# Low parts of the feed-forward gate and up weights made by an accumulating DMA

## The chip, the cores and the metric

The kernel runs on one core of one Trainium2 chip. The metric is the device time of one launch in microseconds; the kernel before took 1728.72 us, the median of three runs.

## The reference

Two layers of an encoder over 512 tokens of 1024 channels. Each layer mixes the tokens in four branches, adds and normalises, and then runs a gated feed-forward network of inner width 2816. The change lies in the feed-forward network alone:

```python
D_FF = ((8 * D_MODEL // 3 + 255) // 256) * 256      # 2816
for l in range(DEPTH):                               # DEPTH = 2
    ...
    x = _layer_norm(DEEPNORM_ALPHA * x + mixed @ w_out[l], ln1_g[l], ln1_b[l])
    ffn = (jax.nn.silu(x @ w_ffn_gate[l]) * (x @ w_ffn_up[l])) @ w_ffn_down[l]
    x = _layer_norm(DEEPNORM_ALPHA * x + ffn, ln2_g[l], ln2_b[l])
```

All operands are float32.

## The kernel before, in words

Every large product is made of three: each float32 operand is split into a high part, rounded to the type fp32r, and a low part, the rest, and TensorE (PE) adds high x high, high x low and low x high in one PSUM bank. The split of a weight tile of 128 x 1024 is done when it is loaded (`wload`, L308): SP issues a DMA into a float32 buffer `wr` (2 buffers), ScalarE (ACT) copies it to `wh` (the high part, 3 buffers), and VectorE (DVE) subtracts, `wl = wr - wh` (3 buffers). `split` (L173) is this pair of instructions. Almost all instructions of the profile carry line 121, that of the recorder through which they are emitted, so groups are told apart by tile names.

The feed-forward network of a layer takes 44 such tiles of `wgu`, gate and up columns in turn. `gemm_t` (L335) makes one tile's product, [128 features, 512 tokens] in the bank `pg`: 24 matmuls, eight with `wh` and XH, eight with `wh` and XL, and the last eight with `wl` and XH, where XH and XL are the two parts of the transposed input. So `wh` is needed from a tile's start, and `wl` from its last third on; the buffer of `wl` is free again when the tile ends. Three PSUM banks turn over: tile n takes the bank of tile n - 3.

The first three tiles (0 to 2) are emitted together by one `gemm_ts`, in two halves of tokens, since the last quarter of the tokens is still being normalised. From tile 3 on each is a `gemm_t` of its own. For each pair f of tiles (gate 2f, up 2f + 1) ACT makes silu of the gate in `fs`, DVE multiplies it by the up product, and the result is split into `gh` and `gl` for the down projection.

GpSimd (POOL) has three kinds of work there. `rows()` (L432), emitted at f = 1: 16 products and sums of 128 x 512 that scale and shift the rows of x for the residual, behind the last square root of the layer norm. In layer 0 alone, `s5_constants` (emitted at f = 0): a chain of small operations on the tables `ea` and `eb`, which begins when ACT has made sines of a table `s5w` of DVE. And, in layer 0 alone, eight times `s5_table` (L290; f = 4, 6, ... 18): six operations of 128 x 512 on `er`, `ei` and `et`, whose results SP stores.

Each engine runs its instructions in the order in which they stand. A scheduler makes that order; what is emitted under `tc.high_priority()` (the splits of weights) is put ahead of other work as soon as it can be placed.

Of the kernel before, what the change touches and what calls it, by code (L numbers as in the profile page):

```python
# [29 lines left out]
# columns of the constant table  # L30
C_ID, C_PERM, C_M, C_MASK, C_IND, C_HALF = 0, 128, 256, 384, 640, 642
C_N = 644
# columns of the per-layer table of per-partition parameters
# [5 lines left out]
# 2 KB slots of SBUF per partition: in general, gates on hold, sums over branches  # L39
# [3 lines left out]
# how work is interleaved: steps between S5's states and its outputs, tiles of gates on hold,  # L43
# backlog of VectorE (us) up to which S5 goes on, assumed latency between engines and of DMA (us)
# [7 lines left out]
class Pace:  # L52
    """a rough clock of the engines, kept while instructions are emitted: what has been emitted
    on each engine until when, and when each tile will be there. It only decides the order in
    which independent work is emitted"""
# [40 lines left out]
    def ring(self, tag, bufs, x):  # L96
        """a tile that takes the place of the one bufs before it"""
        r = self.rings.setdefault(tag, [])
        r.append(x.name)
        if len(r) > bufs:  # L100
            self.last["ring", x.name] = self.last.get(r[-1 - bufs], 0.0) + 0.15

    def ready(self, need):
        """when products of these tiles can start; None: not known yet"""
        if callable(need):
            return need()
        return max([self.when(x) for x in need], default=0.0)


class Metered:  # L110
    """an engine whose instructions advance the clock"""
# [21 lines left out]
def trunk_kernel(ctx: ExitStack, tc: tile.TileContext, xn, xt, wt, w2, wbr, wo, wgu, wdn,  # L133
# [48 lines left out]
    def three(pairs):  # L182
        """the three products of two split operands that carry float32's bits"""
        (ah, al), (bh, bl) = pairs
        return ((ah, bh), (ah, bl), (al, bh))

    # ---------------------------------------------------------------- constants
# [17 lines left out]
    # 0.5 * gate and GLU biases, for sigmoid(z) = (tanh(z/2) + 1) / 2  # L205
    hb = cp.tile([P, L, 36], F32, name="hb")

    # ------------------------------------------------------------------ S5 constants
    def s5_constants(l):
        """of a layer's 8 state tiles: decay, coefficient (exp(lambda dt) - 1) / lambda, and  # L210
        exp(i theta n) for n = 0..31 and n = 32 * (0..15)"""
# [15 lines left out]
        # theta * 2^k, reduced by multiples of 2 pi (exact products of short parts)  # L227
# [39 lines left out]
        # powers of exp(i theta), by doubling  # L267
# [22 lines left out]
    def s5_table(j, tabs):  # L290
        """exp(i theta n), n = 0..511, of a state tile"""
        v3 = lambda a: a.rearrange("p (a b) -> p a b", b=32)
        s3 = [P, 16, 32]
        er, ei, tm, tn = slot("er"), slot("ei"), slot("et"), slot("et")
        ar, ai = (bc(x[:, j, :].unsqueeze(2), s3) for x in tabs[0:2])
        br_, bi_ = (bc(x[:, j:j + 1, :], s3) for x in tabs[2:4])
        G.tensor_tensor(v3(er), ar, br_, ALU.mult)
        G.tensor_tensor(v3(tm), ai, bi_, ALU.mult)
        G.tensor_tensor(er, er, tm, ALU.subtract)
        G.tensor_tensor(v3(ei), ar, bi_, ALU.mult)  # L300
        G.tensor_tensor(v3(tn), ai, br_, ALU.mult)
        G.tensor_tensor(ei, ei, tn, ALU.add)
        return er, ei

    # ------------------------------------------------------------- weight streams
# [16 lines left out]

    def wload_s(src):
        """the same into slots, in halves"""
        hs, ls = [slot("wsh", F32R) for _ in range(2)], [slot("wsl", F32R) for _ in range(2)]
        r = wp.tile([P, 1024], F32, tag="wr", name=nm("wr"), bufs=2)
        pace.ahead = True
        SP.dma_start(r, src)
        with tc.high_priority():
            for i in range(2):  # L330
                split(hs[i], ls[i], r[:, 512 * i:512 * i + 512])
        pace.ahead = False
        return hs, ls

    def gemm_t(src, s, late=None):  # L335
        """[128 features, 512 tokens] = (weight tile)^T x^T, in PSUM"""
        return gemm_ts([src], s, late)[0]

    def gemm_ts(srcs, s, late=None):
        wl = [wload(x) for x in srcs]  # L340
        pss = [mm_ps(s) for _ in srcs]
        for (t0, t1) in (((0, 256), (256, S)) if late else ((0, S),)):
            for i, ((h, l), ps) in enumerate(zip(wl, pss)):
                if late and t0 == 0 and i == len(wl) - 1:
                    late()
                n = 0
                for w, xx in ((h, XH), (h, XL), (l, XH)):
                    for k in range(8):
                        T.matmul(ps[:, t0:t1], w[:, P * k:P * k + P], xx[:, k, t0:t1],
                                 start=(n == 0), stop=(n == 23))  # L350
                        n += 1
        return pss

    def gemm_n(srcs, width, pre=None, late=None):
        """four [128 tokens, width] = x (weight columns), in PSUM"""
# [24 lines left out]
    # ---------------------------------------------------------------- layer norm  # L380
    def layer_norm(l, w_, xh, pss, gt, bt, t, last):
        """x = LN(ALPHA x + psum) of one token tile, in place, the scale and shift left
        out; returns what is to be emitted later: x^T, split, and the scale and shift in rows"""
# [48 lines left out]
        def rows():  # L432
            """the same in rows, for the residual"""
            for h in range(2):
                G.tensor_tensor(xh[h], xh[h], gt[h], ALU.mult)
                G.tensor_tensor(xh[h], xh[h], bt[h], ALU.add)
# [3 lines left out]
    def proj_ln(l, w_, lh, ll, nk, wsrc, kl, ks, xh, gt, bt, last):  # L440
        """x = LN(ALPHA x + a w): a^T split in lh/ll (nk k-tiles), w streamed by rows;
        returns what is left to do for the last token tile"""
# [43 lines left out]
    # -------------------------------------------------------------------- mixers  # L486
    def silu_of(ps):
        """2 * silu, in SBUF"""
# [5 lines left out]
    def head_norm(src, o):  # L494
        """o = src normalised over each 64 of its 512 columns"""
# [93 lines left out]
    def spread(hl, order):  # L589
        """the two parts of a split operand to DRAM, in the order of a stack"""  # L590
# [5 lines left out]
    def fetch(x, r0):  # L596
        """32 rows from r0 of each of three operands, one below the other: one product of 96
        rows then stands for three of 32"""
        r = slot("skr")
        SP.dma_start(r[0:96, :], x[:, r0:r0 + 32, :])  # L600
        return r
# [68 lines left out]
    def gla_in(pss):  # L670
        """evacuate gk | gv | ga of the four token tiles"""
# [11 lines left out]
    def gla(l, gk, ga, gv, qf, gate2, br):  # L683
# [8 lines left out]
        # q * dk^-0.5, split, with the odd / even chunks zeroed  # L692
# [73 lines left out]
    def s5(l, s5c, uspr, br):  # L766
        # input and output matrices: b block-diagonal, c times the coefficient
# [68 lines left out]
        def states(j, cp4, m1, m2, m3, m4):  # L836
# [4 lines left out]
            # x = E y (m1 = re, m3 = im), then split  # L841
# [67 lines left out]
    def spare(*need):  # L909
        """once VectorE has little left to do"""  # L910
        return lambda: max(pace.at["V"] - SPARE, pace.ready(need))

    def gate_stream(l, order, brs, mix):
        """the gated sum over the branches, in steps: tanh(z / 2) of a tile of gates, or, when
        the branch's output is there, its product with the branch's matrix, gated and added"""
# [11 lines left out]
        def branch(bi, i, first, last):  # L927
# [14 lines left out]
            if last:  # L942
                # mixed = acc / 2, split
# [15 lines left out]
        while nb < len(todo):  # L959
# [9 lines left out]
            # matrices of the branches: loaded two pairs of tiles ahead, split one ahead  # L969
# [10 lines left out]
    def run(fill, *gens):  # L980
        """emit the generators' steps: of the first one that TensorE would not wait for,
        otherwise of fill, otherwise of the one that it would wait for least"""
# [17 lines left out]
    # -------------------------------------------------------------------- layers  # L1000
    rest = None
    for l in range(L):
        tt_ = lambda i, s: gemm_t(wt[l, i], s)
        # wt tiles: rq rk rg rg aq aq ak ak gq gr gr su su, then the gates
# [67 lines left out]
        # feed-forward  # L1072
# [3 lines left out]
        for f in range(NF):  # L1076
            if f > 0:
                ps += [gemm_t(wgu[l, i], "pg") for i in range(max(3, 2 * f), 2 * f + 2)]
# [18 lines left out]
# --------------------------------------------------------------- host-side layout  # L1097
def _tiles(w):
    """[.., K, N] -> [.., N/128, 128, K]: per tile of 128 columns, k-tiles side by side"""
# [8 lines left out]
def _constants():  # L1108
# [13 lines left out]
    # rotary tables, [128 = 4 heads x 32, 512]  # L1122
# [3 lines left out]
    # with the retention decay: queries times gamma^n, keys times gamma^-m dk^-0.5  # L1126
# [5 lines left out]
    # what the decay lacks in the blocks of 128 keys and their own 128 queries, [key, head x query]  # L1132
# [6 lines left out]
def _layout(inp):  # L1139
# [20 lines left out]
    wb = _tiles(a["w_branch"])  # [L, 4, 8, 128, 256]  # L1160
# [19 lines left out]
    # attention bias of the last 256 keys of a query tile  # L1180
# [9 lines left out]
    # b: rows = three copies of the 32 channels of tile j, columns [j][re | im][state]  # L1190
    sb = np.zeros((L, 3, 2, 16, 8, 2, 2, 64), f)  # L, copy, group, ch, j, re/im, group, state
    sc = np.zeros((L, 2, 64, 2, 8, 2, 16), f)     # L, group, state, re/im, j, group, ch
# [42 lines left out]
```

## Time and profile before

| | |
|---|---|
| device time, three runs | 1725.30, 1728.72, 1729.99 us |
| span of the profiled execution | 1727.3 us |
| its own device time | not listed apart from the span |
| PE busy | 1667.3 us |
| DVE, ACT, POOL busy | 1000.5, 621.2, 347.6 us |

Times below are microseconds from the start of the span. The feed-forward products of layer 0 run from about 501 to 750, those of layer 1 from 1346 to 1597. A busy entry of PE is a group of matmuls whose ends are modelled, so that consecutive groups overlap a little; the starts are what to read. The number in brackets at the end of a row of the timeline is the idle time of that engine just before it and what ended it.

### The profile page before, as it was taken

What the parts mean: (1) busy time and instruction counts of PE and PEld (TensorE: products, weight loads), DVE (VectorE), ACT (ScalarE), POOL (GpSimd) and SP (SyncE); (2) the same over time, 40 slices, a digit from 0 to 9 for tenths busy, and PEclk for the clock granted to TensorE, in tenths of its full rate; (3) what the DMA queues carried; (4) which work ended last, traced back from release to release, by engine and by line L of the source; (5) the groups of instructions that cost most, each with busy time, mean ns of one, the idle gap of its engine ahead of it and who ended that gap; (6) DMA issues with size and microseconds to landing.
All of it is one profiled execution on the core that took longest, in us unless ns stands there. A gap on an engine that the chain in (4) does not pass through costs nothing. (4 is left out here: it accounts for less than half of the span.)

```text
span 1727.3 us, 19511 instructions
## 1 busy us (share of the span) xinstructions
PE 1667.3 (97%) x7468; PEld 1348.2 (78%) x7468; DVE 1000.5 (58%) x1473; ACT 621.2 (36%) x1012; POOL 347.6 (20%) x363
## 2 busy tenths in 40 slices
PE   8999998889999999999999999999999999999997
PEld 6778786667887888888887788877778888888886
DVE  4667579888577533322374765799875733333225
ACT  4454542233343322221253545433343532222112
POOL 0601025550038921000051000122200600000002
PEclk9998999899999999999999999999999999999999
DMA  6532212222423333322316433133424323322322
GB/s 198 174 108 77 85 61 93 81 88 91 145 94 98 122 122 122 110 98 97 110 61 235 130 99 95 62 119 122 135 80 158 104 92 98 98 87 97 98 98 73
DMA packets 66173, 186.41 MB, mean 108 GB/s; under 512 B 7136, under 2 KB 7328, under 8 KB 66080
## 3 DMA queue, kind: packets, MB, share of 16 engines
q1 hardware_dynamic: 66080, 185.17, 32.8%
q8 instruction: 59, 0.97, 0.2%
q14 instruction: 34, 0.28, 0.0%
HBM read 170.46 MB, written 14.68 MB: 107 GB/s over the span
## 5 line engine op out<-in xcount | busy, mean ns | idle before, releaser
L121 DVE TENSOR_TENSOR wl<-wr,wh 128x1024 fp32r<-128x1024 f32 (+2 forms) x250 | 316.8, 1268 | 537.3 <-PE pg L121 267.7
L121 ACT CAST wh<-wr 128x1024 fp32r<-128x1024 f32 (+2 forms) x250 | 257.5, 1031 | 554.2 <-PE pg L121 240.7
L121 PE MATMUL pg<-XH,wh 128*128 128x512 f32 (+1 forms) x1264 | 316.0, 391 | 1.8 <-DVE fs L121 1.8
L121 PE MATMUL pg<-XL,wh 128*128 128x512 f32 (+1 forms) x1264 | 314.1, 389 | 2.5 <-DVE XL L121 2.5
L121 PE MATMUL pg<-XH,wl 128*128 128x512 f32 (+1 forms) x1264 | 311.2, 388 | 0.0
L121 PEld LDWEIGHTS pg<-XL,wh 128*128 128x128 f32 x1264 | 233.1, 189 | 57.1 <-DVE XL L121 3.3
L121 PEld LDWEIGHTS pg<-XH,wh 128*128 128x128 f32 x1264 | 232.4, 190 | 55.6 <-issue 3.0
L121 PEld LDWEIGHTS pg<-XH,wl 128*128 128x128 f32 x1264 | 232.7, 189 | 54.0
L121 POOL TENSOR_TENSOR rs<-ve,ct 128x1 f32<-128x1 f32 x16 | 10.9, 682 | 727.5 <-DVE ve L121 727.5
L121 PE MATMUL pj<-wl,gh 128*128 128x512 f32 x320 | 102.9, 395 | 0.0
L121 PE MATMUL pj<-wh,gh 128*128 128x512 f32 x320 | 102.7, 394 | 0.0
L121 PE MATMUL pj<-wh,gl 128*128 128x512 f32 x320 | 102.6, 394 | 0.0
L121 POOL TENSOR_TENSOR acc<-acc,sg 128x512 f32<-128x512 f32 x32 | 55.3, 1732 | 170.6 <-DVE sg L121 170.6
L121 ACT CAST gh<-fs 128x512 fp32r<-128x512 f32 x44 | 27.3, 621 | 126.0 <-DVE fs L121 126.0
L121 PEld LDWEIGHTS pj<-wh,gh 128*128 128x128 f32 x320 | 60.3, 188 | 13.8
L121 PEld LDWEIGHTS pj<-wl,gh 128*128 128x128 f32 x320 | 60.3, 188 | 13.7
L121 PEld LDWEIGHTS pj<-wh,gl 128*128 128x128 f32 x320 | 60.3, 188 | 13.4
L121 PE MATMUL gn<-wh,XH 128*128 128x400 f32 (+1 forms) x128 | 49.8, 389 | 5.7 <-ACT XH L121 5.7
L121 ACT ACTIVATE sg<-pg,hb 128x512 f32<-128x512 f32 x64 | 43.9, 686 | 23.4 <-PE pg L121 23.1
L121 DVE TENSOR_TENSOR gl<-fs,gh 128x512 fp32r<-128x512 f32 x44 | 35.1, 797 | 29.7 <-ACT gh L121 29.7
L121 POOL TENSOR_TENSOR hr<-hv,ct 128x8 f32<-128x8 f32 x8 | 13.5, 1687 | 189.6 <-DVE hv L121 189.6
L121 PE MATMUL pb<-brh,bwh 128*128 128x512 f32 x128 | 51.6, 403 | 0.0
(320 smaller groups left out, 2562.2 us busy)
## 6 DMA issues: line engine op xcount, KB each, us to landing
wr<-in_wt SPq DMA_DIRECT2D x90, 512.0 KB
wr<-in_wgu SPq DMA_DIRECT2D x88, 512.0 KB
wr<-in_wdn SPq DMA_DIRECT2D x44, 512.0 KB
bwr<-in_wbr SPq DMA_DIRECT2D x32, 256.0 KB
wr<-in_wo SPq DMA_DIRECT2D x16, 512.0 KB
skr<-spr SPq DMA_DIRECT2D x32, 192.0 KB
wr<-in_w2b SPq DMA_DIRECT2D x8, 400.0 KB
wr<-in_w2a SPq DMA_DIRECT2D x8, 256.0 KB
```

The source lines that it names most:

```text
L121: r = fn(out, *a, **kw)
```

## The change

A new loader `wload_d` is used for the gate and up tiles 3 to 43 of each layer, 82 of 88 in all; tiles 0 to 2 of each layer keep `wload`. In it DVE has no part: ACT copies `wr` to `wh`, then writes `wl = -wh`, and POOL issues a DMA that reads the same weight tile from DRAM once more and adds it to what is in `wl`. POOL issues no DMA in the kernel before.

```diff
+    def wload_d(src):
+
+        r = wp.tile([P, 1024], F32, tag="wr", name=nm("wr"), bufs=2)
+        pace.ahead = True
+        h = wp.tile([P, 1024], F32R, tag="wh", name=nm("wh"))
+        l = wp.tile([P, 1024], F32R, tag="wl", name=nm("wl"))
+        wdma[0] = SP.dma_start(r, src)
+        with tc.high_priority():
+            A.copy(h, r)
+            A.activation(l, h.bitcast(F32), AF.Copy, scale=-1.0)
+            nc.gpsimd.dma_start(l, src, accum_op=ALU.add)
+        pace.ahead = False
+        return h, l
...
-    def gemm_t(src, s, late=None):
-        """[128 features, 512 tokens] = (weight tile)^T x^T, in PSUM"""
-        return gemm_ts([src], s, late)[0]
-
-    def gemm_ts(srcs, s, late=None):
-        wl = [wload(x) for x in srcs]
+    def gemm_t(src, s, late=None, load=None):
+
+        return gemm_ts([src], s, late, load)[0]
+
+    def gemm_ts(srcs, s, late=None, load=None):
+        wl = [(load or wload)(x) for x in srcs]
...
             if f > 0:
-                ps += [gemm_t(wgu[l, i], "pg") for i in range(max(3, 2 * f), 2 * f + 2)]
+                ps += [gemm_t(wgu[l, i], "pg", load=wload_d) for i in range(max(3, 2 * f), 2 * f + 2)]
```

The rest of the diff takes comments out. The order of PE's instructions stays as it is, and that of SP's too but for the stores of `ei`, which stand one place later. Three places show what moves.

POOL at the start of layer 1's feed-forward network, now: the last six of the 16 operations of `rows()` (`x`, with `lg` the scales and `lb` the shifts), then the first of the new DMAs, those of tiles 3 to 6 (`wl_11284` is tile 3's):

```order
L121 TENSOR_TENSOR x_10678<-x_10678,lb_10694 128x512
L121 TENSOR_TENSOR x_10679<-x_10679,lb_10695 128x512
L121 TENSOR_TENSOR x_10680<-x_10680,lg_10690 128x512
L121 TENSOR_TENSOR x_10681<-x_10681,lg_10691 128x512
L121 TENSOR_TENSOR x_10680<-x_10680,lb_10694 128x512
L121 TENSOR_TENSOR x_10681<-x_10681,lb_10695 128x512
L333 DMA wl_11284<-in_wgu 128x1024
L333 DMA wl_11339<-in_wgu 128x1024
L333 DMA wl_11371<-in_wgu 128x1024
L333 DMA wl_11410<-in_wgu 128x1024
```

The first accumulating DMA stands behind all of `rows()`; in layer 0 it does so too, with four small memsets between.

POOL in layer 0 just after that, as a difference: the new DMAs of tiles 3, 4 (`wl_4637`, `wl_4692`) and 5 (`wl_4724`) in the chain of `s5_constants`:

```order
 L121 MEMSET ea_4576 128x8 x2
+L333 DMA wl_4637<-in_wgu 128x1024
+L333 DMA wl_4692<-in_wgu 128x1024
 L121 TENSOR_TENSOR ea_4576<-eb_4575,s5w_4530 128x8
...
 L121 TENSOR_TENSOR ea_4576<-eb_4575,s5w_4530 128x64
 L121 TENSOR_TENSOR eb_4575<-eb_4575,ea_4576 128x8x8
+L333 DMA wl_4724<-in_wgu 128x1024
 L121 TENSOR_TENSOR ea_4576<-eb_4575,s5w_4530 128x64
```

The DMA of tile 5 stands in the middle of the chain, and that of tile 6 behind its end.

POOL further on in layer 0, now: one `s5_table` and the DMAs of tiles 10 (`wl_4917`) to 14 around it; each later table has four DMAs between it and the next:

```order
L333 DMA wl_4917<-in_wgu 128x1024
L121 TENSOR_TENSOR er_4903<-ea_4576,eb_4575 128x512
L333 DMA wl_4949<-in_wgu 128x1024
L121 TENSOR_TENSOR et_4905<-ea_4576,eb_4575 128x512
L121 TENSOR_TENSOR ei_4904<-ea_4576,eb_4575 128x512
L121 TENSOR_TENSOR er_4903<-er_4903,et_4905 128x512
L121 TENSOR_TENSOR et_4906<-ea_4576,eb_4575 128x512
L121 TENSOR_TENSOR ei_4904<-ei_4904,et_4906 128x512
L333 DMA wl_4988<-in_wgu 128x1024
L333 DMA wl_5020<-in_wgu 128x1024
L333 DMA wl_5071<-in_wgu 128x1024
```

Five or six operations of a table now stand ahead of one tile's DMA.

## Rows read from the trace of the kernel before

**Rows 1.** The page's first part: busy time and its share of the span.

```profile
PE 1667.3 (97%) x7468; PEld 1348.2 (78%) x7468; DVE 1000.5 (58%) x1473; ACT 621.2 (36%) x1012; POOL 347.6 (20%) x363
```

**Rows 2.** Busy time by stretch: layer 1, then layer 0, both after the start.

```profile
core 0: us, PE busy (x) PEld busy (x) DVE busy (x) ACT busy (x) POOL busy (x), PEclk, DMA share, GB/s
1367.00:1590.00 223.00, 223.00 (x959) 179.72 (x958) 78.64 (x82) 67.00 (x81) 9.94 (x6) 1.00 0.30 97
556.00:700.00 144.00, 144.00 (x619) 115.41 (x618) 55.94 (x52) 42.49 (x51) 65.48 (x49) 1.00 0.36 115
```

**Rows 3.** Timeline of PE, layer 1: tile 3 by thirds, start of tile 4.

```profile
1367.12 2.02 PE L121 MATMUL pg<-XH,wh 128*128 128x512 f32 x8
...
1370.85 2.03 PE L121 MATMUL pg<-XH,wl 128*128 128x512 f32 x8
1372.71 2.03 PE L121 MATMUL pg<-XH,wh 128*128 128x512 f32 x8
```

**Rows 4.** Timeline of PE, layer 0: tile 3's last third, start of tile 4.

```profile
526.15 2.03 PE L121 MATMUL pg<-XH,wl 128*128 128x512 f32 x8
530.02 2.10 PE L121 MATMUL pg<-XH,wh 128*128 128x512 f32 x8 [1.84 <-DVE fs L121]
```

**Rows 5.** Timeline of POOL, both layers: start, middle and end of the row work.

```profile
526.05 2.52 POOL L121 TENSOR_TENSOR x<-x,lb 128x512 f32<-128x512 f32 x2
528.51 0.15 POOL L121 MEMSET eb<- 128x8 f32 x2
528.58 0.14 POOL L121 MEMSET ea<- 128x8 f32 x2
...
1350.84 2.70 POOL L121 TENSOR_TENSOR x<-x,lg 128x512 f32<-128x512 f32 x2
...
1362.49 3.53 POOL L121 TENSOR_TENSOR x<-x,lg 128x512 f32<-128x512 f32 x2
...
1373.42 3.52 POOL L121 TENSOR_TENSOR x<-x,lb 128x512 f32<-128x512 f32 x2
```

**Rows 6.** Timeline, a weight tile's load in layer 1: issue on SP, first use.

```profile
1363.64 0.33 SPq L121 DMA_DIRECT2D wr<-in_wgu  x1
...
1368.02 1.05 ACT L121 CAST wh<-wr 128x1024 fp32r<-128x1024 f32 x1 [2.01 <-DMA wr<-in_wgu]
```

**Rows 7.** The same in layer 0.

```profile
538.91 0.33 SPq L121 DMA_DIRECT2D wr<-in_wgu  x1
...
542.30 1.05 ACT L121 CAST wh<-wr 128x1024 fp32r<-128x1024 f32 x1 [0.72 <-DMA wr<-in_wgu]
```

**Rows 8.** PE by stretches of 1 us (busy, clock, DMA share, GB/s), around one stall.

```profile
320.00:321.00 1.00, 1.00 (x6) 1.00 1.03 397
...
323.00:324.00 1.00, 0.73 (x4) 1.00 0.00 0
...
328.00:329.00 1.00, 0.26 (x1) 0.50 0.67 262
...
333.00:334.00 1.00, 1.00 (x4) 0.55 0.00 0
334.00:335.00 1.00, 1.00 (x6) 1.00 0.00 0
```

**Rows 9.** Timeline of POOL, layer 0's constants: start, where tile 5's DMA will stand, end.

```profile
534.78 0.20 POOL L121 TENSOR_TENSOR ea<-eb,s5w 128x8 f32<-128x8 f32 x1 [6.05 <-ACT s5w L121]
...
542.94 0.32 POOL L121 TENSOR_TENSOR eb<-eb,ea 128x64 f32<-128x64 f32 x1
...
555.63 0.65 POOL L121 TENSOR_TENSOR ea<-ea 128x64 f32<-128x64 f32 x1
```

**Rows 10.** Groups of DVE and ACT on weight tiles, 1367 to 1590.

```profile
L121 DVE TENSOR_TENSOR wl<-wr,wh 128x1024 fp32r<-128x1024 f32 x41 | 51.9, 1266 | 129.4 <-PE pg L121 129.1 <-ACT wh L121 0.3
L121 ACT CAST wh<-wr 128x1024 fp32r<-128x1024 f32 x41 | 43.2, 1054 | 87.9 <-PE pg L121 85.9 <-DMA wr<-in_wgu 2.0
```

## The prediction, made before the changed kernel ran

> **What bounds the kernel now.** I read the page's busy times first: PE is busy for 97% of the span [rows 1], so only what makes PE wait, or ends a wait of PE, can change the time. The table of stretches shows the feed-forward part in its steady run: in layer 1 PE is busy for 223.00 of 223.00 us and in layer 0 for 144.00 of 144.00, at the full granted clock (1.00, that is 2.4 GHz) [rows 2]. Nothing that leaves DVE there can shorten anything. The timeline of PE gives the beat: a tile takes 5.6 us (1372.71 less 1367.12), and its `wl` is asked for 3.73 us after its start (1370.85) [rows 3]. The one wait of PE that the change could remove is that of 1.84 us before tile 4 of layer 0, for a product of DVE [rows 4].
>
> **What goes away.** 82 subtractions of DVE at 1.27 us (51.9 us for 41) [rows 10], 104 us of DVE work. In the steady run they are hidden behind PE, so I cost their removal at nothing. At the start of layer 0 DVE gets through its work on `s5w` a little sooner, which can save at most the 1.84 us.
>
> **What is added on ACT.** 82 negations of 1024 columns, 1.05 us each by the copy of the same shape [rows 10]: 2.1 us of ACT per tile of 5.6 with the copy. ACT is busy for 67.00 of 223 us now [rows 2], and for about 110 after, so this is hidden. A negation waits until PE has left its buffer, the `wl` of tile n - 3; the copy behind it, of tile n + 1, waits for a later point of PE anyway. SP's loads wait for ACT's copy now instead of DVE's subtraction, which is earlier.
>
> **What is added on POOL and the DMA engines.** 82 DMAs that read 512 KB from DRAM, read 512 KB from SBUF and write it back. No row shows one, so I bound the time from POOL's issue to landing. Below, by a plain load of the same tile: 538.91 to 542.30, 3.4 us [rows 7]; one in layer 1 took 4.4 us (1363.64 to 1368.02) [rows 6]. Above, by two such loads one after the other, 8.8 us. The bytes alone of one pass take 1.4 us: with the 16 engines full (share 1.03) the rate was 397 GB/s [rows 8], and 0.52 MB at 385 GB/s is 1.36 us. I take one load of 4.4 us and one more pass of 1.4 us: 5.8 us, nearest to rows 6, since the operand in SBUF is read beside the other.
>
> The Trainium skill (DMA: Bandwidth & Descriptors, on the anatomy of one DMA on the GpSimd path) gives a DMA issued by GpSimd about 2.0 us plus its bytes at 436 GB/s, which with both operands counted is an estimate of 4.4 us instead of 5.8; by that the sum below would be 2.8 us smaller.
>
> **Steady run: hidden.** Let a tile's negation become possible at time 0, when tile n - 3 ends. `wl` of tile n is asked for two tiles and two thirds later, at 2 x 5.6 + 3.73 = 14.9. The chain is 1.05 (ACT) + 5.8 = 6.9, so 8 us are left. In layer 0 a table of POOL can stand in between: 65.48 us of POOL's time for eight tables [rows 2], 8.2 us each. Then the DMA of tile n + 1 is issued at about 1.05 + 1 + 8.2 = 10.3, lands at 16.1 and is asked for at 20.5: hidden too. The engines' share also fits: plain loads use 0.30 of 5.6 us in layer 1 and 0.36 with the stores of tables in layer 0 [rows 2], 1.7 and 2.0 us per tile; an accumulation at twice the 1.4 us makes 4.5 and 4.8 us of 5.6.
>
> **Start of layer 1: a stall.** This is where the cost lies. The order puts the DMA of tile 3 behind all 16 row operations on POOL. They end at 1376.94 in the trace (1373.42 + 3.52) [rows 5], but partly because DVE's subtractions run beside them: the last pairs take 3.52 us, where a pair without them takes 2.52 [rows 5]. From 1362.49 four pairs are left, so 4 x 2.52 plus about 0.5 for the split of `fs` ends them at 1373.1. The DMA lands at 1373.1 + 5.8 = 1378.9, where PE asks at 1370.85 [rows 3]: **8.05 us**. Today's `wl` is made by DVE, in no queue of POOL. The DMAs of tiles 4 and 5 are issued right behind and have 5.6 us more each, so they follow without a wait.
>
> **Start of layer 0: a stall.** POOL is through with rows and memsets at 528.72 (528.58 + 0.14) [rows 5]; I leave that as it is, since DVE's small `s5w` operations run beside them now and after. The DMA lands at 534.5, tile 3's last third ends 1.87 later, at 536.4, and tile 4 starts there instead of at 530.02 [rows 4]: **6.4 us** (the 1.84 us is swallowed by it). The DMA of tile 5 stands in the chain of constants, which takes 8.5 us up to there (534.78 to 543.26) and 12.9 after [rows 9], about 6 and 9 without DVE's subtractions beside it. The sines that it waits for come some 3 us sooner, at 531, since three of DVE's subtractions (3 x 1.27) no longer stand ahead of their table. So tile 5's DMA is issued at 537 and lands at 543.9, asked for at 536.4 + 5.6 + 3.73 = 545.7; tile 6's is issued at 547.2 and lands at 553 to 554, asked for at 551.3, or 554.2 with the slower clock of the next part. I count nothing for it and keep 2 us for the upper end.
>
> **The clock.** After such a stall PE is slower for a while. The stretches around 324 show it: PE stopped at 323.7, worked again from 328.7 at a granted clock of 0.50 (1.2 GHz), and had 1.00 again only near 333.9 [rows 8]. Some 5.2 us at half speed lose 2.6 us. A stall of like length comes once in each layer: **5.2 us**.
>
> **Sum.** 8.05 + 6.4 + 5.2 = 19.7 us. The profiled span of 1727.3 would become 1747.0. It is 1.4 us under the median of the runs, 1728.72, so I forecast **1748.5 us**. With the lower bound (3.4 us) and no loss of clock it is 5.65 + 4.0 = 9.7, 1738.4; with the upper (8.8), 11.05 + 9.4 + 5.2 + 2, 27.7: 1756.4.
>
> **Rivals.**
> A. The DMA engines become the bound in the steady run. For: an accumulation has three streams, its rate is in no row, and layer 0 has only 3.6 us of engine time per tile left beside 2.0. Against: twice a copy still fits. At 2.5 copies (3.5 us) plus less even use, nearly nothing is added; at 3.5 copies (4.9 us) the pitch is 6.6 us in layer 1 and 6.9 in layer 0, so 41 x 1.0 + 41 x 1.3 = 94 us more, 1843; at 3 copies (4.2 us), 0.3 and 0.6 per tile, 37 us more, 1785.
>
> The Trainium skill (Collectives: The Full Stack, on the bandwidth ceiling) says that an add in the DMA engines reads two sources through one ring and so runs at half the rate of a copy. By that rule an accumulation takes two copies, rival A does not come about, and the time stays with the forecast; no row here shows it.
>
> B. POOL becomes the bound: it has to make the descriptors of each DMA, and no row shows how long that holds it. SP's issue takes 0.33 us [rows 6], which is the one near row and speaks against. It decides from (22.4 - 8.2) / 4 = 3.5 us per DMA in layer 0, and from 5.6 in layer 1. At 5 us it costs 4 x 5 + 8.2 - 22.4 = 5.8 per table, 46 us, with longer first stalls about 1800.
>
> C. Not slower: the first accumulations come in time and only the 1.84 us goes, 1727. It decides if POOL's rows are over by 1370.85 - 5.8 = 1365 and by 520.4. For: without DVE beside it POOL is faster. Against: 16 operations at 1.26 from 1350.84 [rows 5] cannot end before 1371, and the order has nothing that lets the DMA pass them.
>
> **Chances.** Forecast 0.60: the order fixes the stall, and only its length is unknown. A 0.22, B 0.12, C 0.06. About 0.3% (5.2 us) is what a measurement of this kernel can tell from no change. Slower: 0.60 + 0.22 + 0.12 = 0.94; C is 0.05 no change and 0.01 faster. The range is 1737 to 1805: the forecast's own 1738 to 1756, then the lower half of A and B; above it are the rest of A and some of B, below it C.
>
> **What would show it.** In the profile after, POOL should show its first accumulation behind the rows in both layers, PE a wait for a DMA into `wl` of 6 to 9 us in tile 3 of each layer and a clock of 0.5 behind it, and then 5.6 us per tile with PE never idle, the DMA share rising from 0.30 to 0.7 or 0.9. Wrong in the way of A: a pitch over 5.6 us in layer 1 with a DMA share near 1. Of B: a pitch over 5.6 with POOL busy or held in its DMAs. Of C: no wait of PE for `wl`.

## The result, and the profile after

The changed kernel takes **1752.66 us**, the median of four runs (1750.48 to 1754.26), against 1729.36 us (1725.30 to 1730.63) for the kernel before on the same chip: a ratio of 1.0125, with a 95% interval of 1.0103 to 1.0147. It is slower by 23.3 us; the forecast was 19.8 us slower.

The page's first part for the kernel after, which answers to [rows 1]:

```profile
span 1748.7 us, 19736 instructions
...
PE 1672.1 (96%) x7468; PEld 1352.6 (77%) x7468; DVE 931.7 (53%) x1391; ACT 698.7 (40%) x1094; POOL 397.0 (23%) x445
```

ACT has gained 78 us and POOL 49. DVE has lost 69 us and not the 104 at which its subtractions were priced (by the two pages that group fell by 108 us, from 316.8 to 209.0); the last section tells where most of the rest is. The span does not follow from these sums. PE is busy only 4.8 us longer, so most of the 21.4 us by which the span grew is time in which PE stood.

Where it stood is read from PE's timeline. Layer 1 first, which answers to [rows 3]: tile 3 by thirds, then tile 4.

```profile
1377.23 2.02 PE L121 MATMUL pg<-XH,wh 128*128 128x512 f32 x8
1379.09 2.03 PE L121 MATMUL pg<-XL,wh 128*128 128x512 f32 x8
1389.01 3.78 PE L121 MATMUL pg<-XH,wl 128*128 128x512 f32 x8 [7.89 <-DMA wl<-in_wgu]
1392.59 3.05 PE L121 MATMUL pg<-XH,wh 128*128 128x512 f32 x8
```

PE reaches the last third of tile 3 and waits 7.89 us for `wl`. The next two groups of eight matmuls take 3.78 and 3.05 us where 2.03 is usual. The stretches of 1 us around it (busy, granted clock, DMA share, GB/s) show why, as [rows 8] did for an earlier stall:

```profile
1384.00:1385.00 1.00, 0.00 (x0) 0.80 0.83 299
1385.00:1386.00 1.00, 0.00 (x0) 0.50 1.04 119
...
1393.00:1394.00 1.00, 1.00 (x4) 0.50 0.27 49
1394.00:1395.00 1.00, 1.00 (x4) 0.58 0.00 0
1395.00:1396.00 1.00, 1.00 (x6) 1.00 0.40 45
```

The granted clock falls to 0.50 (1.2 GHz) while PE stands, and is 1.00 (2.4 GHz) again only in 1395.

POOL's timeline there answers to [rows 5] and gives the reason of the wait:

```profile
1380.64 2.49 POOL L121 TENSOR_TENSOR x<-x,lb 128x512 f32<-128x512 f32 x2
1383.08 2.66 POOL L333 DMA_DIRECT2D wl<-in_wgu  x3
1394.22 0.87 POOL L333 DMA_DIRECT2D wl<-in_wgu  x1 [8.48 <-ACT wl L121]
```

The first accumulating DMA is issued at 1383.08, right behind the last row operation, and lands when PE goes on: 1389.01 less 1383.08 is 5.9 us.

Layer 0, which answers to [rows 4], has two waits, at tile 3 and at tile 6:

```profile
529.06 3.78 PE L121 MATMUL pg<-XH,wl 128*128 128x512 f32 x8 [7.17 <-DMA wl<-in_wgu]
532.64 2.96 PE L121 MATMUL pg<-XH,wh 128*128 128x512 f32 x8
...
551.09 3.25 PE L121 MATMUL pg<-XH,wl 128*128 128x512 f32 x8 [2.42 <-DMA wl<-in_wgu]
554.14 2.48 PE L121 MATMUL pg<-XH,wh 128*128 128x512 f32 x8
```

POOL's issues of tiles 3 and 4, of tile 5, and of tiles 6 and 7:

```profile
523.47 1.96 POOL L333 DMA_DIRECT2D wl<-in_wgu  x2
...
533.29 0.88 POOL L333 DMA_DIRECT2D wl<-in_wgu  x1 [0.15 <-issue]
...
544.10 1.79 POOL L333 DMA_DIRECT2D wl<-in_wgu  x2 [0.15 <-issue]
```

After that nothing waits. Two long stretches, which answer to [rows 2] (the columns are the same):

```profile
570.00:710.00 140.00, 140.00 (x602) 112.80 (x601) 45.59 (x26) 65.11 (x76) 61.69 (x62) 1.00 0.87 210
1400.00:1590.00 190.00, 190.00 (x816) 153.10 (x815) 23.49 (x34) 88.12 (x103) 29.36 (x34) 1.00 0.82 188
```

PE is busy for all of both at the full clock, DVE does in layer 1 about a third of what it did (23.49 of 190 us, against 78.64 of 223), and the 16 DMA engines are busy for 0.82 and 0.87 of the time instead of 0.30 and 0.36.

One measure serves for all that follows: the time from the start of tile 3 to the first matmul of the down projection (group `pj`), both from PE's timeline. It holds 41 tiles, and 41 x 5.6 us = 229.6 us is the least that PE needs.

| kernel | layer 0, us | layer 1, us |
|---|---|---|
| before | 231.68 | 229.59 |
| after | 243.80 | 240.38 |

The change costs 12.12 + 10.79 = 22.9 us in these two parts, which is the whole of the measured 23.3. What stands outside them differs between executions by some us either way: tile 3 of layer 0 starts at 522.42 in the profile of before and at 518.00 in that of after, though the first load that was changed is that of tile 3 itself. The kernel before ran from 1723.87 to 1740.57 us in 25 runs on the chip of the first group of experiments.

### The profile page after: what moved, and what is told of

Its sections match the earlier page's. It is cut to its first block, busy times and chain, and to the rows that moved or that the text cites. A ratio compares the mean times of both kernels' runs of the same rounds, so it can differ in the third digit from the quotient of the medians.

```text
span 1748.7 us, 19736 instructions
## 1 busy us (share of the span) xinstructions
PE 1672.1 (96%) x7468; PEld 1352.6 (77%) x7468; DVE 931.7 (53%) x1391; ACT 698.7 (40%) x1094; POOL 397.0 (23%) x445
## 3 DMA queue, kind: packets, MB, share of 16 engines
q0 software_dynamic: 11808, 43.00, 14.5%
## 5 line engine op out<-in xcount | busy, mean ns | idle before, releaser
L121 DVE TENSOR_TENSOR wl<-wr,wh 128x1024 fp32r<-128x1024 f32 (+2 forms) x168 | 209.0, 1246 | 306.3 <-ACT wh L121 227.3
L121 PE MATMUL pg<-XH,wl 128*128 128x512 f32 (+1 forms) x1264 | 315.9, 393 | 17.5 <-DMA wl<-in_wgu 17.5
L121 PE MATMUL pg<-XH,wh 128*128 128x512 f32 (+1 forms) x1264 | 320.0, 395 | 0.0
L121 PEld LDWEIGHTS pg<-XH,wh 128*128 128x128 f32 x1264 | 236.3, 193 | 54.3 <-issue 0.7
L121 DVE TENSOR_TENSOR fs<-fs,pg 128x512 f32<-128x512 f32 x44 | 30.2, 687 | 310.7 <-PE pg L121 310.7
L333 POOL DMA_DIRECT2D wl<-in_wgu x82 | 71.6, 890 | 299.8 <-ACT wl L121 289.3
L121 ACT ACTIVATE wl<-wh 128x1024 fp32r<-128x1024 f32 x82 | 87.0, 1060 | 81.8 <-PE pg L121 81.7
L121 DVE TENSOR_TENSOR gl<-fs,gh 128x512 fp32r<-128x512 f32 x44 | 69.9, 1589 | 39.5 <-ACT gh L121 39.5
```

What stands on the lines that cost most here:

```text
L121: r = fn(out, *a, **kw)
L333: nc.gpsimd.dma_start(l, src, accum_op=ALU.add)
```

## The experiments

The theory: an accumulation costs nothing while it is issued in time; the loss is the issue behind other work of POOL at the start of each layer's feed-forward part, with the lower clock behind each stall. The rivals: it costs something all along, by the DMA engines (A) or by POOL (B).

**Accumulations from tile 10 on, in both layers.**

```diff
-load=wload_d) for i in ...
+load=wload_d if i >= 10 else None) for i in ...
```

> Tiles 3 to 9 of each layer get their low parts from VectorE again, tiles 10 to 43 (68 of 82) keep the accumulating DMA. Theory (the cost lies in TensorE's waits for the first accumulations, 7.2 and 2.4 us in layer 0 and 7.9 us in layer 1, with the slower clock behind them): all waits of TensorE for a DMA into wl are gone, the time is that of the kernel before within 5 us, 1725 to 1734 us. Rival (the accumulations cost something in the steady run as well, by load on the DMA engines or on GpSimd): 68 of 82 of a spread cost of 23 us stay, 1744 to 1750 us.

Measured: 1731.70 us (1727.58 to 1735.20, ten runs), ratio 0.9992 (0.9973 to 1.0012). PE has no wait for a `wl` of the accumulating loader. The parts take 233.45 and 229.60 us; the 1.8 us more than before in layer 0 stand at the old wait for `fs`, which is 2.09 us here with 1.6 us of slower clock behind it. 68 of the 82 accumulations are left and cost nothing that can be measured, though the DMA share is 0.80 in the steady run of layer 1. So the steady run is not where the time goes.

**The same in layer 0 alone.**

```diff
+load=wload_d if l or i >= 10 else None) for i in ...
```

> Only layer 0's tiles 3 to 9 go back to VectorE; layer 1 is as in the changed kernel. Theory: layer 0's share goes (waits of 7.2 and 2.4 less the old wait of 1.8, and 4.3 us of slower clock, 12 us), layer 1's 10.6 us stay: 1738 to 1744 us, one wait for a DMA into wl of 7 to 9 us. Rival (cost spread over the run): 1748 to 1753 us.

Measured: 1740.14 us (1736.81 to 1745.88, ten runs), ratio 1.0047 (1.0023 to 1.0071). The one wait for `wl` left is that of layer 1, 7.64 us. By the medians the stall of layer 1 alone costs 1740.14 less 1731.70 = 8.4 us (9.3 by its part, 238.88 less 229.60), and the two of layer 0 cost 1752.66 less 1740.14 = 12.5 (10.4 by the part, 243.80 less 233.45).

**The row work put off.** All 82 accumulations stay; `rows()` is emitted at f = 8, behind the accumulating DMA that was issued last.

```diff
-            if f == 1:
-                rows()
+            if f == 8:
+                rows(gdma[0].ins)
```

> All 82 accumulations stay; GpSimd's 16 row operations of each layer are put behind the accumulation of tile 17. Theory (the row work ahead of the first accumulation is what delays it): in layer 0 the first accumulation is issued near 520 and lands near 526, so tile 3's wait is under 1 us; tile 6, behind the chain of constants, may still wait up to 2 us; layer 1 has no wait; 1726 to 1737 us. Rival (the first accumulations are late for a reason of their own: their landing, the engines' load, ScalarE's negation): waits of 5 us or more stay, 1744 us or more.

Measured: 1737.06 us (1732.84 to 1742.67, ten runs), ratio 1.0029 (1.0006 to 1.0051), just past the upper edge of the range. The waits at tile 3 shrink to 1.88 and 1.10 us, where under 1 us and none had been expected, and that at tile 6 is gone. What is left at tile 3 does not come from work ahead of the DMA on POOL: POOL stood still for 11.55 us until ACT's negation was there, issued at 515.15, 2.2 us before tile 3 began, and the DMA took 7.9 us to land (in layer 1 11.14 and 7.1 us). By these 1 to 2 us the rival, which named the negation and the landing, is right. And a new wait of 2.8 us came up in each layer where the row work now stands. POOL and PE of this kernel in layer 0:

```profile
610.44 1.64 POOL L121 TENSOR_TENSOR x<-x,lb 128x512 f32<-128x512 f32 x1
612.02 1.80 POOL L334 DMA_DIRECT2D wl<-in_wgu  x2
```

```profile
617.36 2.56 PE L121 MATMUL pg<-XH,wl 128*128 128x512 f32 x8 [2.86 <-DMA wl<-in_wgu]
619.71 3.18 PE L121 MATMUL pg<-XH,wh 128*128 128x512 f32 x8
```

POOL's order there is one accumulation (601.58), seven row operations, then the next two (612.02), with nine more row operations ahead of the first. So DMAs are late in the middle of the steady run, and the stall moved with its cause. Something else was gained that nobody asked for: the waits of PE for DVE's `x` and `XL` ahead of tile 3 are gone. That is followed up below.

**One more transfer per tile.** In the changed kernel SP also stores every float32 tile to DRAM, where nobody reads it.

```diff
+        more.append(more.pop(0))
+        nc.sync.dma_start(more[-1], r)
```

> The changed kernel with one more DMA per tile, a store of the 512 KB weight buffer to DRAM, which nothing reads. Theory (the steady run is hidden because the DMA engines' time, 3.1 us per accumulation and 1.6 per load, fits in 5.6 us per tile): with 1.6 us more, 6.2 in layer 1 and 6.5 in layer 0, the engines become the bound; the tile takes 6.2 to 6.6 us, DMA share near 1, and the time rises by 25 to 75 us to 1778 to 1828 us. Rival (engines are far from their limit, the packets' times overlap): the tile stays at 5.6 us and the time within 6 us of the changed kernel's 1752.

Measured: 1777.89 us (1776.34 to 1779.44, two runs), ratio 1.0253 (1.0201 to 1.0305), just under the range. Its parts take 263.22 and 245.05 us, 24.1 us more than in the kernel after. Two stretches of its steady run:

```profile
570.00:710.00 140.00, 134.46 (x570) 106.35 (x569) 39.72 (x22) 58.90 (x68) 57.51 (x56) 1.00 0.95 262
1430.00:1590.00 160.00, 160.00 (x687) 128.17 (x686) 18.65 (x27) 70.29 (x81) 23.39 (x27) 1.00 0.97 261
```

In layer 1 the engines are at 0.97 and PE never stands in this stretch: the tile stays at 5.6 us, where 6.2 had been expected. The waits of layer 1 come ahead of it (9.87 us at tile 3) and behind it (three of 0.52 to 1.07 us from 1605 on). In layer 0, with the stores of the tables on top, PE loses 5.5 of 140 us to waits for `wl`. So rival A is real, but no share at which it begins can be read from this run: from 570 to 640 PE does not stand at 0.96, and from 640 to 700 it loses 4.4 us at 0.93. In its own steady run the changed kernel, at 0.82 and 0.87, has no such wait.

**The add taken away.** POOL issues a plain load of the same tile instead, so `wl` holds the whole weight and this kernel leaves out the low part.

```diff
-            nc.gpsimd.dma_start(l, src, accum_op=ALU.add)
+            nc.gpsimd.dma_start(l, src)
```

> The changed kernel with POOL's DMA as a plain load instead of an accumulating one, 82 times: wl is then the whole weight and not its low part, so a part of the computation is changed; the work of all engines but the DMA engines is the same. It prices the add. Theory (the add is a second pass over the tile): the median from issue to landing falls from 5.4 us to 4.0 to 4.6, the 16 DMA engines spend about 1.56 us on it instead of 3.09 (share in the steady run of layer 1 from 0.82 to about 0.55), and the two first stalls get about 1 us shorter each (7.17 and 7.89 now), the one of tile 6 (2.42) also: span 1743 to 1747. Rival (a DMA of POOL is slow whatever it does): landing stays at 5.2 to 5.5 us, share near 0.8, and the stalls stay as they are, 1747 to 1752.

Measured: one run of 1751.75 us, span 1750.0, at the place where the rival stood; the theory's 1743 to 1747 missed. By its parts the theory holds: the waits for `wl` are 5.32, 1.84 and 6.51 us instead of 7.17, 2.42 and 7.89, and the feed-forward parts take 238.73 and 238.36 us, 7.1 us less than in the kernel after. What ate this in the span lies outside them (tile 3 of layer 0 starts at 525.45 instead of 518.00, and from the last part to the end it takes 135.2 us instead of 131.1), and one execution can't tell it from the scatter. The price of the add is plain. Queue, engine group and landing of the kernel after (packets, MB, share of the 16 engines; KB each and median us from issue to landing):

```profile
q0 software_dynamic: 11808, 43.00, 14.5%
L333 POOL DMA_DIRECT2D wl<-in_wgu x82 | 71.6, 890 | 299.8 <-ACT wl L121 289.3
wl<-in_wgu POOLq DMA_DIRECT2D x82, 512.0 KB, 5.4
```

and of the kernel with the plain load:

```profile
q0 software_dynamic: 11808, 43.00, 7.8%
L333 POOL DMA_DIRECT2D wl<-in_wgu x82 | 45.0, 549 | 317.7 <-ACT wl L121 317.4
wl<-in_wgu POOLq DMA_DIRECT2D x82, 512.0 KB, 3.6
```

An accumulation takes 14.5% of 1748.7 us, or 3.09 us of all 16 engines per tile, against 1.66 for the plain load: 1.86 times. It lands after 5.4 instead of 3.6 us (4.0 to 4.6 had been expected of the plain load), and holds POOL for 0.89 instead of 0.55 us. The two rows of queue q0 show the same 43.00 MB: the bytes don't tell the second operand, only the time does.

**Tile 6 of layer 0 alone by the old loader.** The forecast had put its wait at nothing.

```diff
+load=wload_d if l or i != 6 else None) for i in ...
```

> The changed kernel with tile 6 of layer 0 alone by the old loader. Theory (tile 6's DMA is late because it stands behind the chain of constants, and it alone): PE's wait of 2.42 us there and the 1.63 us of clock behind it go, the waits at tile 3 (7.17 and 7.89) stay, 1752.7 - 4.1 = 1748 to 1749. Rival (the constants make the next ones late too): tile 7 takes over with a wait of 1 to 2 us, 1751 to 1753.

Measured: 1747.80 us (1744.87 to 1751.49, five runs), ratio 1.0094 (1.0072 to 1.0116), 0.2 us under the range. Layer 0's part takes 238.97 us, 4.8 less than after. PE's waits for `wl` in the whole kernel (us in total, times, longest):

```profile
PE pg L121 <- DMA wl<-in_wgu: 15.7, 2, 8.4
```

These are the ones at tile 3 of each layer, 7.25 and 8.41 us; tile 7 has none. The theory holds: that one DMA stood behind the chain of constants, and it alone.

**The row work in four parts.** Tile 3 by the old loader, accumulations from tile 4 on, and the row work of one token tile (four operations) at each of f = 9, 11, 13 and 15.

```diff
-            if f == 1:
-                rows()
+            if f in (9, 11, 13, 15):
+                rows(gdma[0].ins, [(f - 9) // 2])
```

> The changed kernel with tile 3 by the old loader (accumulations from tile 4 on, 80 of them) and the row work in four parts, at f = 9, 11, 13 and 15, each behind the latest accumulating DMA. Theory (the whole price of the change is what stands ahead of a DMA on POOL): the waits for wl that were left with the row work in one piece at f = 8 (1.88, 1.10, 2.86, 2.79) go, and with them about 3 us of clock: 1720 to 1726. Rival (accumulations in the steady run cost something beyond POOL's order, by the 16 engines' share of 0.8 and more): 1731 to 1738.

Measured: 1722.83 us (1718.97 to 1732.43, twelve runs), ratio 0.9962 (0.9946 to 0.9978). The feed-forward parts take 230.31 and 229.60 us: 80 accumulations with a single wait of 0.44 us. With POOL's queue put in order, and tile 3 left to DVE, 0.7 us of the loss is left in the parts, and the kernel is faster than the one before. Is that the accumulations' doing, or the row work's?

**The kernel before with the row work put off**, and no accumulation at all: at f = 3, behind a small operation that reads `gl`.

```diff
+            if f == 3:
+                an = sm.tile([P, 1], F32, tag="an", name=nm("an"))
+                rows(G.tensor_tensor(an, l_.bitcast(F32)[:, 0:1], l_.bitcast(F32)[:, 0:1], ALU.add).ins)
```

> The kernel before, without any accumulating DMA, with the row work of POOL put off to f = 3, behind a small POOL operation that reads gl. It asks whether the row work costs the kernel before something by itself. Theory (POOL's row work slows DVE beside it at the start of each feed-forward part, as the run with the row work at f = 8 suggests, where PE's waits for x and XL are gone): PE's waits for DVE's x and XL (4.6 us in both layers) and for fs (1.84) go, 1727.3 - 6.4 = about 1721 in the profile, ratio 0.994 to 0.998. Rival (these waits are of DVE's own chain, or move to the place of the row work): 1727 to 1731, ratio 0.999 to 1.001.

Measured: 1722.78 us (1720.07 to 1724.83, six runs), ratio 0.9952 (0.9937 to 0.9967). The waits for `x` and `XL` and that of 1.84 us [rows 4] are gone, as expected. A new one came up in layer 0, of which the expectation knew nothing: PE waits 4.88 us for `fs` at 584.20. SP's queue shows where from:

```profile
552.90 0.33 SPq L121 DMA_DIRECT2D wr<-in_wgu  x1
577.02 0.33 SPq L121 DMA_DIRECT2D esp<-er  x1
577.44 0.38 SPq L121 DMA_DIRECT2D wr<-in_wgu  x1
```

The row work delays POOL's tables; SP issues nothing from 553 to 577, until the store of `er`, whose last operation on POOL ends at 576.99; the next weight load stands behind that store. ACT's copy of that tile waits for the load until 580.90, DVE's subtraction waits for the copy, and the product with `fs` that PE needs stands behind the subtraction. A late piece of POOL reached PE through the queues of SP, ACT and DVE.

**The kernel before with the row work in four parts**, at f = 9, 11, 13 and 15.

> The kernel before, without any accumulating DMA, with the row work in four parts at f = 9, 11, 13 and 15, each behind a small POOL operation that reads gl. With the row work in one piece at f = 3 the tables of layer 0 came late, SP's queue stood behind their stores from 552.9 to 577.0, and PE waited 4.88 us for fs. Theory (in four parts the tables are in time; what the row work cost is all that there is to gain, with or without the accumulations): the 4.88 us and about 2 us of clock go, 1714 to 1719, ratio 0.991 to 0.995. Rival (the accumulations have a part in the time of the run with four parts, by DVE's 104 us): 1722 to 1728, above that run's 1722.8.

Measured: **1718.20 us** (1715.14 to 1721.25, six runs), ratio 0.9929 (0.9908 to 0.9949), the fastest of all. Its feed-forward parts take 229.59 and 229.60 us, which is the floor, and PE has no wait for `fs`, `x`, `XL` or `wl` in them or ahead of them. The rival, that the accumulations had a part in the gain, falls: without them the parts are no longer, and the time is no worse. Why the version with accumulations is 4.6 us above this one is open (the two were measured on different chips, and the intervals of their ratios, 0.9946 to 0.9978 and 0.9908 to 0.9949, just overlap); its parts are only 0.7 us longer, and its profiled execution was the longest of its twelve (1732.43), so what lies outside can't be compared.

**The loader in another place.** The feed-forward tiles by the old loader, the 64 tiles of gates in the mixing part by the new one.

```diff
-            pg = gemm_t(wt[l, 13 + 8 * bi + i], "pg")
+            pg = gemm_t(wt[l, 13 + 8 * bi + i], "pg", load=wload_d)
```

> The accumulating loader used in another place: all feed-forward tiles by the old loader, the 64 tiles of gates in the mixing part by the new one. There DVE is what PE waits for (busy for 86.6 of 100 us between 300 and 400 of the kernel before, PE for 85.2). If DVE's load sets these waits, 64 subtractions of 1.27 us less (81 us of DVE) shorten the 26 us of PE's waits for DVE in the mixing part: 1705 to 1722. Rival (POOL's order again: its sums of acc wait for products of DVE, and the DMAs queue behind them): new waits of PE for wl, 1740 to 1800.

Measured: 1752.55 us (1750.77 to 1756.49, four runs), ratio 1.0126 (1.0104 to 1.0149). The theory fell, and the rival's mechanism with it, though the time lies in the rival's range: PE has no wait for `wl`. What grew, in PE's waits (us in total, times, longest):

```profile
PE sv L121 <- ACT stk L121: 14.5, 6, 5.8
...
PE sg L121 <- ACT swgh L121: 11.1, 2, 5.6
PE sy L121 <- ACT xrh L121: 7.4, 2, 4.7
PE pg L121 <- DVE sg L121: 5.4, 4, 3.0
```

In the kernel before the first of these was 8.5 us and the next two were not there. Whether the negations on ACT did this isn't shown: the planner's clock of the engines sees other costs, and it wrote another order for the whole mixing part. The cause stays open.

## Why the prediction was right, and where it was off

**What bounds the kernel, and the steady run: right.** PE is busy throughout at 1.00, the pitch stays at 5.6 us, and removal and addition of 82 pieces of work are hidden. The run with accumulations from tile 10 on shows it by itself for 68 of them.

**The price of an accumulation: right.** 5.8 us were taken between 3.4 and 8.8. At the two places that count it was 529.06 - 523.47 = 5.6 and 5.9; the median of all is 5.4. The two terms of the working were off against each other: POOL's plain load lands in 3.6 us, where 4.4 were taken for it, and the add puts 1.8 us on that instead of 1.4. So the nearness of the sum is in part luck. The fit of the Trainium skill (DMA: Bandwidth & Descriptors, on the anatomy of one DMA on the GpSimd path), which had given an estimate of 4.4, is 1.0 us under that median.

**Layer 1's stall: right.** 8.05 us forecast, 7.89 measured, behind the row work as said and for the reason given: without DVE's subtractions beside it the row work ends 5.85 us after the start of tile 3 (1383.08 less 1377.23), where the working had 5.98 and the kernel before 9.82.

**Layer 0's stall at tile 3: right in kind, 1.1 us too long.** 6.4 us were forecast, net of the old 1.84; the wait is 7.17, net 5.3. The end of the row work was taken from the trace of before as it stood there, 6.30 us after the start of tile 3; it came after 5.47 (523.47 less 518.00). In the kernel before one row operation ran beside a subtraction of DVE here too (517.54, 2.28 us, where its neighbours take 1.29), and that subtraction went with the change. The DMA was 0.2 us shorter than taken.

**The clock: right, with luck.** 2.6 us were taken for each of the two stalls. The thirds from the late one to the next tile's second take 1395.47 - 1389.01 = 6.46 us instead of 3.73, which loses 2.7; in layer 0 it is 2.65. The same measure in other runs gives 1.5, 2.0 and 2.5 us behind stalls of 7.64, 7.25 and 8.41 us. Behind shorter stalls it is sometimes 1.6 and sometimes next to nothing: 1.6 behind the 1.88 us at tile 3 of layer 0 in the run with the row work put off, 0.1 behind the 2.79 us in its layer 1, where the granted clock stays at 1.00.

**Tile 6 of layer 0: the term that was mis-sized.** "I count nothing for it and keep 2 us for the upper end." It waits 2.42 us and loses 1.64 of clock behind that (551.09 to 556.46, less 3.73): 4.1 us. The working had the landing 18.5 to 19.5 us after that of tile 3 and the request 19.7 after it (554.2 less 534.5): a us of room at most, behind a long chain of small operations. (Of tile 5 it says issued at 537 and landed at 543.9; with 5.8 us that is 542.8. Nothing hangs on it.) The request came as worked out, 19.6 us after tile 3's landing (551.09 less 2.42, less 529.06). Measured, the landing comes 22.0 us after tile 3's (551.09 - 529.06). Of the 3 us between 19.0 and 22.0, 1.7 are the start of the chain (tile 5's issue 4.2 instead of 2.5 us after tile 3's landing), 0.6 the chain, and 0.7 the DMA, which takes 7.0 us with two more right behind it. A term with so little room should have been counted, in part at least. The run with tile 6 alone on the old loader took 4.9 us off.

**The sum.** 7.17 - 1.84 + 2.65 + 2.42 + 1.64 in layer 0 and 7.89 + 2.73 in layer 1 make 22.7, against the forecast 19.7 and the 22.9 of the parts.

**Rival A** was refused for the right reason. The forecast took twice a copy, 2.8 us of the engines; the add was measured at 1.86 plain loads, 3.09 us. The shares of 4.5 and 4.8 of 5.6 us came out too: that is 0.80 and 0.86, against 0.82 and 0.87. The rule of the Trainium skill that was weighed there (Collectives: The Full Stack, on the bandwidth ceiling) said half the rate, which this nearly is. The room left was small: one more store per tile filled the engines to 0.95 and 0.97. **Rival B** fell: POOL is held for 0.89 us per accumulation, far from the 3.5 at which it would have begun. **Rival C** fell with the order, as argued.

**What the prediction did not see** is that the row work, at the same place, already cost the kernel before something: that kernel takes 12 us more than its version with the row work in four parts (1730.19 less 1718.20). Of these 2.1 stand in layer 0's part and 4.6 in waits for `x` and `XL` ahead of both parts; the rest isn't placed.

## What to carry to other kernels

Work that is moved to an idle engine is priced not by that engine's load but by what stands ahead of it in its queue at the one moment when it is late: here 68 of 82 transfers were free together, and three that were issued late cost 23 us. A stall of a few us on TensorE is to be counted with the stretch at the lower clock behind it: here 1.5 to 2.7 us behind 7 to 8 us, and between next to nothing and 1.6 behind 2 to 3. Before an engine is relieved, look at whether its slow stretch comes from its own load or from a neighbour's work at the same time: putting off 16 operations of GpSimd gained 0.7%, and taking two thirds of VectorE's work out of the steady run gained nothing.

## What was not expected of the hardware

POOL's row work slows DVE beside it far more than the 2.52 and 3.52 us of [rows 5] had told of POOL itself. DVE's timeline at the start of layer 0's feed-forward part, in the kernel before, beside the row work:

```profile
505.95 2.91 DVE L121 TENSOR_SCALAR x<-x,mv,rs 128x512 f32<-128x512 f32 x2 [0.44 <-POOL rs L121]
...
511.76 3.43 DVE L121 TENSOR_TENSOR XL<-xf,XH 128x512 fp32r<-128x512 f32 x2
...
518.59 5.02 DVE L121 TENSOR_SCALAR s5w<-th 128x8 f32<-128x8 f32 x7
523.64 5.37 DVE L121 TENSOR_SCALAR s5w<-s5w 128x72 f32<-128x72 f32 x5
```

and the same instructions in the fastest version, where the row work stands later:

```profile
504.60 1.00 DVE L121 TENSOR_SCALAR x<-x,mv,rs 128x512 f32<-128x512 f32 x2 [0.44 <-POOL rs L121]
...
508.54 1.29 DVE L121 TENSOR_TENSOR XL<-xf,XH 128x512 fp32r<-128x512 f32 x2 [0.38 <-ACT XH L121]
...
513.57 0.60 DVE L121 TENSOR_SCALAR s5w<-th 128x8 f32<-128x8 f32 x7
514.21 1.13 DVE L121 TENSOR_SCALAR s5w<-s5w 128x72 f32<-128x72 f32 x5
```

Seven operations on eight columns take 5.02 us in place of 0.60. Seen one by one, four of the seven take 1.26 or 1.27 us and three 0.16, about what each takes in the fastest version (0.16 or 0.17). One of the four in the kernel before, with the row operation beside it:

```profile
519.79 1.28 POOL L121 TENSOR_TENSOR x<-x,lg 128x512 f32<-128x512 f32 x1
519.84 1.26 DVE L121 TENSOR_SCALAR s5w<-th 128x8 f32<-128x8 f32 x1
```

Each of the four ends 0.02 to 0.03 us after a row operation of POOL: their time is that of the neighbour and not of their own size. It is counted as busy, so DVE's busy time hides it. The Trainium skill (SBUF — State Buffer, on the two separate sides) says that the two engines share a pair of ports under an exclusive lock, held for a whole instruction; these rows agree, since an end that goes with the neighbour's instruction and not with the operation's own size is what such a lock would make.

Most of the DVE time that did not go away, 35 us, is of the same kind. In the changed kernel the split `gl` has the following durations (min, median, max in ns; start of the first and the last in us):

```profile
L121 DVE TENSOR_TENSOR gl<-fs,gh x44: 691/693/6530, 526.4 to 1620.4; 128x512 fp32r<-128x512 f32 x44
```

Its total rose from 35.1 to 69.9 us. All of that is in layer 0, between 560 and 770, where POOL makes its tables: 19 of them take 52.3 us there, 2.75 each, and in layer 1 they take 0.69. Six of the 19 take 6.43 to 6.53 us and nine 0.69. Each of the six begins 0.3 us before a table, and runs until the sixth of the table's operations has begun; the longest, with the first and the last of them:

```profile
707.64 6.53 DVE L121 TENSOR_TENSOR gl<-fs,gh 128x512 fp32r<-128x512 f32 x1 [0.90 <-ACT gh L121]
707.97 1.39 POOL L121 TENSOR_TENSOR er<-ea,eb 128x512 f32<-128x512 f32 x1
...
713.69 1.63 POOL L121 TENSOR_TENSOR ei<-ei,et 128x512 f32<-128x512 f32 x1
```

No operation of a table takes over 1.63 us there, so DVE lost its turn several times in a row. In the kernel before, a `gl` met two operations of a table at most and took 1.18 to 1.43 us. Here it cost nothing, since PE does not wait for `gl`; but a 0.7 us operation of DVE beside a table of POOL can become nine times as long.
